# Retention gates by one Silu activation, and five pieces of a hybrid decoder kernel put elsewhere in the order of issue

## The chip, the cores and the metric

The kernel runs as one program on one core of a Trainium2 chip. The metric is the device time of an execution in microseconds (us). It is shown as the median of several runs. A profiled execution has a time of its own, beside the span from its first to its last instruction. The engines are TensorE (PE, with the weight loads as PEld), VectorE (DVE), ScalarE (ACT), GpSimd (POOL) and SyncE (SP). Each runs its own queue of instructions in order. An instruction waits on semaphores until what it needs is there, and everything behind it on its engine waits with it.

## The reference, cut to what matters

Two layers on x of 512 tokens by 1024 features, in float32. In each layer one projection makes the operands of two mixers and of two gates:

```python
h = rmsnorm(x, g_mix)
z = h @ w_in
aq, ak, av, rq, rk, rv, rg, ga, gb = jnp.split(z, SPLIT_POINTS, axis=-1)

aq = rope_half(aq.reshape(B, S, N_Q_HEADS, HEAD_DIM), pos)
ak = rope_half(ak.reshape(B, S, N_KV_HEADS, HEAD_DIM), pos)
ya = sliding_window_sink_attention(aq, ak, av, sinks) @ w_a

r = chunkwise_retention(rq, rk, rv)
r = r * lax.rsqrt(jnp.mean(r * r, axis=-1, keepdims=True) + EPS)
r = r.reshape(B, S, RET_V) * jax.nn.silu(rg.astype(jnp.float32))
yb = r.astype(x.dtype) @ w_b

mixed = jax.nn.sigmoid(ga) * ya + jax.nn.sigmoid(gb) * yb
x = x + mixed @ w_out
h2 = rmsnorm(x, g_mlp)
x = x + jnp.square(jax.nn.relu(h2 @ w_up)) @ w_down
```

Attention has 8 query heads over 2 key heads of 64, in bands of 128 queries, with a learned sink in the softmax. A last RMSNorm ends the program.

## The kernel before

Everything is kept transposed: features lie on the partitions and the 512 tokens along the free axis. A float32 matrix is brought to TensorE as two parts, a high one that ScalarE rounds (L342 for weights, L417 for values) and a low one that VectorE gets as the difference (L343 and L418). A product of two such operands is three matmuls, high by high (L394), low by high (L395) and high by low (L396). The weights come in units of 128 x 1024 that SyncE loads (`raw`) and `split_until` splits, `SPLIT` = 3 units ahead of the one in use. So the splits are spread through the queues of ScalarE and VectorE between all other work.

One layer goes through these stages. The projection in chunks of 128 features (`mm`), with attention's keys and queries first. `rotate` turns each (L638, L639, then L642 to L644 with tables that L633 scales by the row's norm); where its last argument is true, ScalarE first copies the bank of the result (L641), so that L642 reads the copy and not the bank. Then attention in four groups of two heads per key head and band, interleaved with the projection's other chunks: scores (L780), masked maximum (L788), exponential (L800), the sink's exponential (L803), scaling (L807), transposition of the weights (`pT`, L745), and the product with v (`pv`, L765 and L766), whose halves L767 and L768 put into `whole`. In the projection's chunks for the retention gate (`rg`), `put_rg` makes `z`, and `silu` applies the activation to it, eight times in a layer: four pieces at the end of attention, and four in the fast multiplication that makes the rest of the gates. Retention runs as a generator, `retention(pair)`, for two heads at a time: scores, outputs, norm and finish are steps between which other work is issued. The MLP is in blocks e of 512 hidden features, by a fast multiplication that uses sums and differences of operands (`sums`, `eu`, `b`); its result goes to memory by `Adding.put`, which adds the piece on VectorE (L1662) or sends it.

The order on each engine is set in three ways. The code issues chunks of the projection, and `advance` draws in a step of the background work (attention, retention) with each half of a chunk. A scheduler then places the instructions on each engine by priority as their operands and buffers come free. And `tc.issue_after(i)` holds what is issued in its block behind the named instruction i. `last_split` is the last split of attention's result (`whole`) into its halves, and `last_exp` the last exponential of the sink.

Three places are touched most. The tail of attention (L1176 to L1183): behind the last exponential `x`, which holds the gates a and b there, is passed through a sigmoid (L1178, two of 128 x 2048, with a table load), then come the first two `silu`; the other two come behind the last split. The keys of layer 1 (`put_k`, L671), where the bank of k's result is read by L642. The first MLP block, e = 0 (L1822 to L1824), where `rest` issues the last sum of inputs (L544) and its split (L417, L418) right after the block is issued.

Of the kernel before, what the change touches and what calls it, by code (L numbers as in the profile page):

```python
# [12 lines left out]
AF = mybir.ActivationFunctionType  # L13
ALU = mybir.AluOpType
# [38 lines left out]
SPLIT = 3  # L53
# [63 lines left out]
def decoder(ctx, tc, xT, x_first, w_in, w_rg, w_rv, w_a, w_b, w_wo, w_up, w_pair, w_down, w_end, tables, decay, band, g_last, out):  # L117
    nc = tc.nc
# [10 lines left out]
    def f32(ap):  # L129
        return ap.bitcast(F32)  # L130

    def temp(name="t"):
        return tmp.tile([P, T], F32, tag="t", name=name, bufs=7)

    def big(name, dtype=F32):
        return tmp.tile([P, 2, T], dtype, tag="big", name=name, bufs=6)
# [28 lines left out]
    state = {"next": 0, "loaded": 0, "split": 0, "hold": None}  # L165

    def halves(i):

        return (slice(0, UNIT // 2), slice(UNIT // 2, UNIT)) if i < 3 else (slice(0, UNIT),)
# [11 lines left out]
    def load_until(n):  # L181
        while state["loaded"] < min(n, len(order)):
            i = state["loaded"]
            layer, name, j = order[i][:3]
            if name == "pair":
                load_part(i)
            elif name == "block":
                load_block(i)
            elif name in MIXING:
                load_values(i)  # L190
            else:
                raws[i] = raw_tile()
                for at in halves(i):
                    queue = nc.scalar if i == 0 and at.start == 0 else nc.sync
                    source = w_end[j] if name == "w_end" else weights[name][layer, j]
                    queue.dma_start(raws[i][:, at], source[:, at])
                    if i < 3:
                        load_x()
            state["loaded"] += 1
# [79 lines left out]
    def add_part(i):  # L279
        if order[i][3] in (1, 2):  # L280
            last = raws.pop(i - 1)
            at = LEFT if order[i][3] == 1 else RIGHT
            nc.vector.tensor_tensor(raws[i][:, at], last[:, LEFT], last[:, RIGHT], ALU.add)  # L283
# [18 lines left out]
    def add_block(i):  # L302
        e, part = order[i][2:]
        if part in (2, 4) and e < N_BLOCK - 1:
            raws[i] = raws.pop(i - 2)
            nc.vector.tensor_tensor(raws[i], raws[i], raws.pop(i - 1), ALU.add)
# [10 lines left out]
    def add_values(i):  # L317
        name, part = order[i][1:3]
        if part in (2, 4):
            n = TALL[name]  # L320
            raws[i] = raws.pop(i - n)
            nc.vector.tensor_tensor(raws[i], raws[i], raws.pop(i - 2 * n), ALU.add)

    def split_until(n):
        while state["split"] < min(n, len(order)):
            i = state["split"]
            name, part = order[i][1], order[i][-1]
            if name in MIXING:
                add_values(i)
            load_until(i + AHEAD)  # L330
            if name == "pair":
                add_part(i)
            elif name == "block":
                add_block(i)
            raw = raws[i]
            hi = wpool.tile([P, UNIT], F32R, tag="hi", name="hi", bufs=SPLIT + 1)
            lo = wpool.tile([P, UNIT], F32R, tag="lo", name="lo", bufs=SPLIT + 1)
            for at in (LEFT,) if name == "pair" and part == 3 else halves(i):
                if i == 0 and at.start == 0:
                    nc.vector.tensor_copy(hi[:, at], raw[:, at])  # L340
                else:
                    state["high"] = nc.scalar.activation(hi[:, at], raw[:, at], AF.Copy).ins  # L342
                nc.vector.tensor_tensor(lo[:, at], raw[:, at], f32(hi[:, at]), ALU.subtract)  # L343
            kept = {
                "pair": part < 2,
                "block": name == "block" and part < 4 and order[i][2] < N_BLOCK - 1,
                **{n: name == n and order[i][2] < 4 for n in MIXING},
            }
            if not kept.get(name):
                raws.pop(i)  # L350
            parts[i] = (hi, lo)
            state["split"] += 1
# [268 lines left out]
    def layer_body(layer):  # L621
# [14 lines left out]
        def rotate(ps, tabs, early=False):  # L636
            a, b = temp("rot"), temp("rot2")
            nc.scalar.activation(b[0:64, :], ps[64:128, :], AF.Copy)  # L638
            nc.scalar.activation(b[64:128, :], ps[0:64, :], AF.Copy)  # L639
            if early:  # L640
                nc.scalar.activation(a, ps, AF.Copy)  # L641
            nc.vector.tensor_tensor(a, a if early else ps, tabs[0], ALU.mult)  # L642
            nc.vector.tensor_tensor(b, b, tabs[1], ALU.mult)
            nc.vector.tensor_tensor(a, a, b, ALU.add)  # L644
            return a
# [11 lines left out]
        attn_tabs, v_box = [], []  # L657
# [8 lines left out]
        def beside(g, stack, src):  # L666
            for s in range(2):
                own, other = 64 * s + 32 * g, 64 * s + 32 - 32 * g
                nc.sync.dma_start(f32(stack)[other : other + 32, :], f32(src)[own : own + 32, :])

        def put_k(ps):  # L671
            r = rotate(ps, attn_tabs, layer == 0)
            lo = big("klo")[:, 0, :]
            for g in range(N_KV):
                nc.scalar.activation(kh[g], r, AF.Copy)
            nc.vector.tensor_tensor(lo, r, f32(kh[0]), ALU.subtract)
            for g in range(N_KV):
                nc.vector.tensor_scalar(kl[g], lo, half[:, g : g + 1], None, ALU.mult)
                beside(g, kh[g], kh[g])
# [306 lines left out]
        rg, rg_next = {}, {}  # L986
# [71 lines left out]
            done(1)  # L1058

        def silu(i):  # L1060
            s = temp("sig")
            nc.scalar.activation(s, rg[i], AF.Sigmoid)
            nc.vector.tensor_tensor(rg[i], rg[i], s, ALU.mult)

        ret = {}

# [69 lines left out]
        def load_decay(pair):  # L1136
            decays[pair] = big("dm")
            nc.sync.dma_start(decays[pair], decay[:, 2 * pair : 2 * pair + 2, :])

        def retention(pair):  # L1140
            two = [Head(2 * pair), Head(2 * pair + 1)]
            for head in two:
                for js in ((0, 1), (2, 3)):
                    head.scores(js)
                    yield
            two[0].outputs(0)
            yield
            two[0].outputs(1)
            yield
            two[1].outputs(0)  # L1150
            yield
            yield
            two[0].norm()
            yield
            two[1].outputs(1)
            yield
            yield
            yield
            two[1].norm()
            if pair == 0:  # L1160
                load_decay(1)
            yield
            yield
            for head in two:
                head.finish()
                yield
# [9 lines left out]
        with tc.issue_after(last_exp[0]):  # L1176
            for hs in (slice(0, T // 2), slice(T // 2, T)):
                nc.scalar.activation(x[:, :, hs], x[:, :, hs], AF.Sigmoid)  # L1178
            for i in range(2):
                silu(i)  # L1180
        with tc.issue_after(last_split[0]), tc.issue_after(last_split[1]):
            for i in range(2, 4):
                silu(i)  # L1183
        turned.take()
# [7 lines left out]
        for u in range(4):  # L1192
            hi, lo = unit("w_a", layer)
            for j in range(2):
                c = 2 * u + j
                ps = bank(ps_mm, "mm")
# [447 lines left out]
        class Adding:  # L1644
# [14 lines left out]
            def put(self, i, j, m, ps, sign):  # L1659
                t = self.kept.pop((i, j, m), None)  # L1660
                if t is not None:
                    nc.vector.scalar_tensor_tensor(t, ps, self.scale(j, m, sign), t, ALU.mult, ALU.add)  # L1662
                else:
                    t = self.evacuated(j, m, temp("y"), ps, sign)
                self.send(i, j, m, t, last or self.e > 0)
# [138 lines left out]
        rest = []  # L1804
        for e in range(N_BLOCK):
            if e == 0:
                into = Adding(e)
                hooks = first_hooks()
                for c in (0, 2):
                    two_chunks("w_up", layer, xs, [put_up(c), put_up(c + 1)], hooks[c // 2])  # L1810
            else:
                plain = last and e == N_BLOCK - 1
                into = Ending() if e == N_BLOCK - 1 else Adding(e)
                if last and e == 2:
                    with tc.issue_after(state["high"]):
                        nc.scalar.activation(sq[:, 0:1], factor[:, 0:1], AF.Sqrt)
                pair(0)
                pair(1)
            if last and e == N_BLOCK - 1:
                down_plain(into)  # L1820
            else:
                down(e, into, None if e else lambda: rest.append(sum_input(2)))  # L1822
                if e == 0:
                    rest.pop()()  # L1824
        u_forms.free()
        slots.give(*u_two_slots, *u_one)

# [182 lines left out]
```

## Time and profile before

| what | value |
|---|---|
| median of three runs | 1462.46 us (1461.82 to 1465.33) |
| profiled execution | 1464.44 us |
| its span, first to last instruction | 1462.5 us |
| granted TensorE clock, mean | 0.999 |
| matmuls, us in them | 8185, 1449.4 |
| activations and loads on ScalarE | 974.0 us |
| VectorE | 1182.1 us |
| table loads on ScalarE | 17 of 1.283 us |

The profiled execution lies 1.98 us above the median of the three runs, and its span is 1.94 us shorter than its own time; all rows that follow are from this one execution. In its lists a row gives the start, the length and the instruction; behind "<-" stands what the engine waited for. The profile gives the time that an engine sat idle before an instruction in brackets. The pitch of matmuls, from one start to the next, shows what a wait cost better than the idle time alone does.

### The profile page before, as it was taken

To read this page: it belongs to the slowest core of one execution; us is meant where nothing else is said; L and a number is where in the kernel's file an instruction comes from. 1 tells how busy PE (TensorE), PEld (TensorE's weight loads), DVE (VectorE), ACT (ScalarE), POOL (GpSimd) and SP (SyncE) were. 2 spreads that over 40 slices of the span, in tenths; PEclk is the share of its full clock that TensorE was granted. 3 is DMA by queue.
4 is the path that set the end of the run, shared out by engine and by line. 5 is a ranking of instruction groups with operands and counts; after the bars stand their busy time and mean duration, and the time that the engine had idled before them with its cause. 6 is when DMAs were issued, how large, how long until landed. Compare 5 with 4: busy or idle time off the path is not lost.

```text
span 1462.5 us, 22466 instructions
## 1 busy us (share of the span) xinstructions
PE 1449.4 (99%) x8185; PEld 1270.0 (87%) x8185; DVE 1182.1 (81%) x1776; ACT 974.0 (67%) x1590; POOL 226.6 (15%) x335
## 2 busy tenths in 40 slices
PE   9999999999999999999999999999999999999998
PEld 7888888888988999999888889888889889999997
DVE  6978887867898888888778789878689888888885
ACT  6656665544687777777756576555447877777775
POOL 0011002222101111111201110012210011111120
PEclk9999999999999999999999999999999999999999
DMA  7598249999735777666955983599975477777664
GB/s 258 176 293 236 88 154 299 285 279 270 221 109 196 195 193 196 168 177 179 310 175 175 289 240 121 161 311 263 278 182 183 139 195 198 197 189 199 173 192 142
DMA packets 97294, 302.83 MB, mean 207 GB/s; under 512 B 11424, under 2 KB 11552, under 8 KB 90784
## 3 DMA queue, kind: packets, MB, share of 16 engines
q0 software_dynamic: 36512, 129.78, 37.9%
q1 hardware_dynamic: 59952, 170.32, 33.9%
q8 instruction: 64, 1.05, 0.3%
q10 hardware_dynamic: 720, 1.31, 0.2%
q14 instruction: 46, 0.38, 0.1%
HBM read 261.78 MB, written 120.06 MB: 261 GB/s over the span
## 4 chain that ended last, share of the span: by engine, by line
PE 96%; DVE 2%; ACT 1%; DMA 1%; issue 0%; DVEq 0%
PE mm L395 22%; PE mm L394 22%; PE mm L396 22%; PE wo L1354 5%; PE rg L1015 3%; PE b L394 3%; PE b L395 3%; PE b L396 3%; PE rv L395 2%; PE rv L394 2%; PE rv L396 2%; PE mm L410 2%; PE score L780 1%; PE pT L745 1%; PE r L395 1%; PE r L396 1%
## 5 line engine op out<-in xcount | busy, mean ns | idle before, releaser
L342 ACT ACTIVATE hi<-raw 128x1024 fp32r<-128x1024 f32 (+1 forms) x393 | 400.2, 1021 | 244.9 <-PE mm L395 122.3
L343 DVE TENSOR_TENSOR lo<-raw,hi 128x1024 fp32r<-128x1024 f32 (+1 forms) x394 | 460.2, 1176 | 96.4 <-ACT hi L342 93.0
L394 PE MATMUL mm<-xh,hi 128*128 128x512 f32 (+1 forms) x912 | 319.1, 354 | 1.6 <-DVE rot L642 0.6
L395 PE MATMUL mm<-xl,hi 128*128 128x512 f32 (+1 forms) x912 | 319.6, 353 | 0.0
L396 PE MATMUL mm<-xh,lo 128*128 128x512 f32 (+1 forms) x912 | 316.4, 353 | 0.5 <-DVE lo L343 0.5
L394 PEld LDWEIGHTS mm<-xh,hi 128*128 128x128 f32 x912 | 173.1, 190 | 25.6 <-ACT xh L420 1.2
L395 PEld LDWEIGHTS mm<-xl,hi 128*128 128x128 f32 x912 | 173.3, 190 | 21.9
L396 PEld LDWEIGHTS mm<-xh,lo 128*128 128x128 f32 x912 | 172.3, 190 | 21.8 <-DVE lo L343 0.7
L395 PE MATMUL mm<-r,hi 128*128 128x256 f32 (+1 forms) x608 | 189.3, 311 | 0.8 <-DVE r L418 0.8
L396 PE MATMUL mm<-r,lo 128*128 128x256 f32 (+1 forms) x608 | 189.0, 311 | 0.0
L394 PE MATMUL mm<-r,hi 128*128 128x256 f32 (+1 forms) x608 | 186.6, 312 | 0.5 <-ACT mm L1529 0.5
L394 PEld LDWEIGHTS mm<-r,hi 128*128 128x128 f32 x608 | 115.5, 190 | 9.9 <-ACT r L417 1.1
L395 PEld LDWEIGHTS mm<-r,hi 128*128 128x128 f32 x608 | 115.7, 190 | 9.6 <-DVE r L418 1.6
L396 PEld LDWEIGHTS mm<-r,lo 128*128 128x128 f32 x608 | 115.8, 190 | 6.3
L1677 POOL DMA_DIRECT2D y<-eu x56 | 63.0, 1397 | 372.2 <-DVE eu L1662 371.9
L395 PE MATMUL mm<-lo,r 128*128 128x512 f32 (+1 forms) x276 | 104.3, 387 | 0.0
L396 PE MATMUL mm<-hi,r 128*128 128x512 f32 (+1 forms) x276 | 100.9, 387 | 0.0
L394 PE MATMUL mm<-hi,r 128*128 128x512 f32 (+1 forms) x276 | 98.3, 389 | 0.3 <-ACT r L417 0.2
L394 PE MATMUL b<-hi,r 128*128 128x512 f32 x180 | 70.6, 392 | 1.9 <-DVE eu L1662 1.9
L283 DVE TENSOR_TENSOR raw<-raw 128x512 f32<-128x512 f32 x56 | 38.6, 690 | 41.2 <-DMA raw<-w_pair_in 35.1
L395 PE MATMUL b<-lo,r 128*128 128x512 f32 x180 | 70.2, 390 | 0.0
L1354 PE MATMUL wo<-r,hi 128*128 128x256 f32 x384 | 69.2, 283 | 0.0
(337 smaller groups left out, 2870.9 us busy)
## 6 DMA issues: line engine op xcount, KB each, us to landing
raw<-w_in_in SPq DMA_DIRECT2D x65, 512.0 KB, 5.5
sums_down<-w_down_in POOLq DMA_DIRECT2D x30, 1024.0 KB, 12.9
sums_up<-w_pair_in POOLq DMA_DIRECT2D x56, 512.0 KB, 12.0
raw<-w_down_in SPq DMA_DIRECT2D x45, 512.0 KB, 7.5
raw<-w_pair_in SPq DMA_DIRECT2D x84, 256.0 KB, 3.6
y<-y POOLq DMA_DIRECT2D x62, 256.0 KB, 9.9
y<-eu POOLq DMA_DIRECT2D x61, 256.0 KB, 8.7
raw<-sums_down SPq DMA_DIRECT2D x30, 512.0 KB, 7.7
```

Source lines behind the costliest of these rows:

```text
L283: nc.vector.tensor_tensor(raws[i][:, at], last[:, LEFT], last[:, RIGHT], ALU.add)
L342: state["high"] = nc.scalar.activation(hi[:, at], raw[:, at], AF.Copy).ins
L343: nc.vector.tensor_tensor(lo[:, at], raw[:, at], f32(hi[:, at]), ALU.subtract)
L394: nc.tensor.matmul(ps, ah, bh, start=start and i == 0, stop=False, **more)
L395: nc.tensor.matmul(ps, ah, bl, start=False, stop=False, **more)
L396: latest[0] = nc.tensor.matmul(ps, al, bh, start=False, stop=stop and i == n - 1, **more).ins
L410: latest[0] = nc.tensor.matmul(ps, w[:, cols(j, c)], moving[k][low], start=first, stop=bool(final)).ins
L745: nc.tensor.transpose(pt[:, i * P : (i + 1) * P], sm[:, at : at + P], ident)
L780: nc.tensor.matmul(ps[:, g * w : (g + 1) * w], q_s[g][:, c, at], part[:, keys], start=i == 0, stop=i == 1)
L1015: nc.tensor.matmul(o, w[:, cols], v, start=start and k == 0 and n == 0 and w is hi and v is vh, stop=k == 3 and n == 1 and w is lo, skip_g ...
L1354: latest[0] = nc.tensor.matmul(o, w[:, cols], v, start=start and first and n % 2 == 0 and w is hi and v is vh, stop=final and w is lo, ski ...
L1677: nc.gpsimd.dma_start(y[:, 2 * j + m, i * T : (i + 1) * T], t, **how)
```

## The change

There are five edits. `silu` becomes one activation in place, Silu, where a Sigmoid and a multiplication stood. In the tail of attention, one more unit of weights is split behind the last split of attention, ahead of the last two `silu`. In `retention`, the norm of the first two heads comes after the fourth head's outputs, not between third and fourth. `put_k` passes True, so that the bank of the keys is copied in layer 1 too, where only layer 0 did it before. And `Adding.put` keeps the addition in `self.added`, and the last sum of the first MLP block is issued behind it.

```diff
         def put_k(ps):
-            r = rotate(ps, attn_tabs, layer == 0)
+            r = rotate(ps, attn_tabs, True)
...
         def silu(i):
-            s = temp("sig")
-            nc.scalar.activation(s, rg[i], AF.Sigmoid)
-            nc.vector.tensor_tensor(rg[i], rg[i], s, ALU.mult)
+            nc.scalar.activation(rg[i], rg[i], AF.Silu)
...
             two[1].outputs(0)
             yield
             yield
-            two[0].norm()
-            yield
             two[1].outputs(1)
             yield
+            two[0].norm()
             yield
             yield
             two[1].norm()
...
         with tc.issue_after(last_split[0]), tc.issue_after(last_split[1]):
+            split_until(state["next"] + SPLIT + 1)
             for i in range(2, 4):
                 silu(i)
...
             def put(self, i, j, m, ps, sign):
                 t = self.kept.pop((i, j, m), None)
                 if t is not None:
-                    nc.vector.scalar_tensor_tensor(t, ps, self.scale(j, m, sign), t, ALU.mult, ALU.add)
+                    self.added = nc.vector.scalar_tensor_tensor(
+                        t, ps, self.scale(j, m, sign), t, ALU.mult, ALU.add
+                    ).ins
...
                 if e == 0:
-                    rest.pop()()
+                    with tc.issue_after(into.added):
+                        rest.pop()()
```

These edits move the order of instructions at several places. In the rows, numbers behind a name are those of buffers; they differ between the two programs. Line numbers behind the edits shift by two or three.

On ScalarE at the keys of layer 1, the bank of k, `mm_7310` before and `mm_7294` after, is read by L638 and L639. Before:

```order
L638 ACTIVATE rot2_7534<-mm_7310 64x512
L639 ACTIVATE rot2_7534<-mm_7310 64x512
L417 ACTIVATE sh_7490<-wide_7488 128x512
L342 ACTIVATE hi_7583<-raw_7444 128x1024
L342 ACTIVATE hi_7629<-raw_7450 128x1024
L616 ACTIVATE rstd_7524<-ssq_7525 128x512
```

And after:

```order
L638 ACTIVATE rot2_7518<-mm_7294 64x512
L639 ACTIVATE rot2_7518<-mm_7294 64x512
L641 ACTIVATE rot_7517<-mm_7294 128x512
L417 ACTIVATE sh_7474<-wide_7472 128x512
L638 ACTIVATE rot2_7538<-mm_7296 64x512
L639 ACTIVATE rot2_7538<-mm_7296 64x512
L342 ACTIVATE hi_7568<-raw_7428 128x1024
```

The copy L641 now stands right behind L639, and the rotation of the next chunk, `mm_7296`, comes ahead of two splits of weights.

On VectorE in the first MLP block of layer 0, L1662 (L1660 after) adds the four evacuated pieces `eu`. Before:

```order
L544 SCALAR_TENSOR_TENSOR sums_4148<-sums_4147,xg_4144 128x512
L418 TENSOR_TENSOR r0_81<-sums_3989,r0_81 128x512
L283 TENSOR_TENSOR raw_4154<-raw_4122 128x512
L343 TENSOR_TENSOR lo_4125<-raw_4023,hi_4124 128x1024
L418 TENSOR_TENSOR r1_82<-sums_4147,r1_82 128x1024
L343 TENSOR_TENSOR lo_4157<-raw_4078,hi_4156 128x1024
L1662 SCALAR_TENSOR_TENSOR eu_4140<-mm_4074,columns_3899,eu_4140 128x512
L418 TENSOR_TENSOR r4_85<-sums_4148,r4_85 128x1024
L1662 SCALAR_TENSOR_TENSOR eu_4142<-mm_4075,columns_3899,eu_4142 128x512
L1662 SCALAR_TENSOR_TENSOR eu_4118<-b_4076,columns_3899,eu_4118 128x512
L1662 SCALAR_TENSOR_TENSOR eu_4120<-b_4077,columns_3899,eu_4120 128x512
```

And after:

```order
L418 TENSOR_TENSOR r1_82<-sums_4131,r1_82 128x1024
L343 TENSOR_TENSOR lo_4141<-raw_4062,hi_4140 128x1024
L1660 SCALAR_TENSOR_TENSOR eu_4124<-mm_4058,columns_3883,eu_4124 128x512
L1660 SCALAR_TENSOR_TENSOR eu_4126<-mm_4059,columns_3883,eu_4126 128x512
L1660 SCALAR_TENSOR_TENSOR eu_4102<-b_4060,columns_3883,eu_4102 128x512
L343 TENSOR_TENSOR lo_4165<-raw_4082,hi_4164 128x1024
L1660 SCALAR_TENSOR_TENSOR eu_4104<-b_4061,columns_3883,eu_4104 128x512
L544 SCALAR_TENSOR_TENSOR sums_4132<-sums_4131,xg_4128 128x512
L343 TENSOR_TENSOR lo_4189<-raw_4106,hi_4188 128x1024
L343 TENSOR_TENSOR lo_4212<-raw_4138,hi_4211 128x1024
L283 TENSOR_TENSOR raw_4208<-raw_4184 128x512
L418 TENSOR_TENSOR r4_85<-sums_4132,r4_85 128x1024
```

The sum (L544) and its split, `r4_85`, now stand behind the last of the four.

On ScalarE at the end of attention in layer 1, from the last exponential of the sink (L803) on. Here `x_75` holds the two gates, `z` with `sig` or alone the retention gate, `whole` the result of attention, and `pT` the transposed weights. Before:

```order
L803 ACTIVATE st_8400<-st_8400 128x2
L1178 ACT_TABLE_LOAD
L1178 ACTIVATE x_75<-x_75 128x8x256 x2
L417 ACTIVATE late_7390<-rot_8447 128x512
L767 ACTIVATE whole_8411<-pv_8412 64x512
L767 ACTIVATE whole_8411<-pv_8419 64x512
L1062 ACTIVATE sig_8634<-z_8505 128x512
L417 ACTIVATE r3_84<-pT_8428 128x4x128
L1062 ACTIVATE sig_8637<-z_8505 128x512
L342 ACTIVATE hi_8648<-raw_8507 128x1024
L417 ACTIVATE r6_87<-whole_8411 128x4x128
L417 ACTIVATE r3_84<-pT_8467 128x4x128
```

And after:

```order
L803 ACTIVATE st_8385<-st_8385 128x2
L1175 ACT_TABLE_LOAD
L1175 ACTIVATE x_75<-x_75 128x8x256 x2
L1061 ACT_TABLE_LOAD
L1061 ACTIVATE z_8490<-z_8490 128x512 x2
L417 ACTIVATE r6_87<-whole_8396 128x4x128
L417 ACTIVATE late_7374<-rot_8432 128x512
L638 ACTIVATE rot2_8655<-mm_8629 64x512
L639 ACTIVATE rot2_8655<-mm_8629 64x512
L417 ACTIVATE r3_84<-pT_8452 128x4x128
L417 ACTIVATE r3_84<-pT_8471 128x4x128
L417 ACTIVATE r3_84<-pT_8511 128x4x128
```

The Silu of the first two pieces stands with a table load right behind the gates, and the halves of `pT` come behind more work; the weight split `hi_8648` and the two halves of `whole` are no longer between them. On TensorE, 82 matmuls of 512 columns and 16 of 128 stand from the last scores to the next product with v there before, and 56 and 16 after; the seven chunk matmuls that stood between the last product with v and the retention matmuls behind it stand ahead of that product now.

The program's table loads become 21.

## The prediction

> **What bounds the kernel now.** I read the page first, for the engine shares and the chain that ended last, then TensorE's waits, then the timelines around each wait and around the places that the change reorders. Three lines of the page:
>
> ```profile
> span 1462.5 us, 22466 instructions
> PE 1449.4 (99%) x8185; PEld 1270.0 (87%) x8185; DVE 1182.1 (81%) x1776; ACT 974.0 (67%) x1590; POOL 226.6 (15%) x335
> PE 96%; DVE 2%; ACT 1%; DMA 1%; issue 0%; DVEq 0%
> ```
>
> TensorE is busy for 99% of the span and is 96% of the chain. Its work isn't touched: it has 8185 matmuls and keeps them. So the change can gain only what TensorE waits for, and lose only by making it wait elsewhere. VectorE, at 81%, and ScalarE, at 67%, matter only where they are late. The waits of TensorE (total us, times, longest) are these:
>
> ```profile
> PE b L394 <- DVE eu L1662: 1.9, 2, 1.2
> PE mm L394 <- DVE rot L642: 0.6, 1, 0.6
> ```
>
> Few microseconds are to be had. A wait is larger in the pitch of the matmuls than in this list, since the first matmul behind it runs longer, so I count by start times. A matmul of 512 columns starts every 0.227 us in an undisturbed stretch, one of 256 columns every 0.12, one of 128 every 0.11; these three come from the starts in the stretches below and beside them.
>
> **The Silu itself.** Sixteen sigmoid activations become sixteen Silu activations, and sixteen multiplications go.
>
> ```profile
> L1062 ACT ACTIVATE sig<-z 128x512 f32<-128x512 f32 x16 | 9.3, 620 | 1.1 <-DVE z L1034 1.0
> L1063 DVE TENSOR_TENSOR z<-z,sig 128x512 f32<-128x512 f32 x16 | 10.6, 685 | 0.1
> ...
> 852.73 1.28 ACT L1178 ACT_TABLE_LOAD   x1
> ```
>
> On VectorE 10.6 us of work go. That is no gain of time by itself, because TensorE waits for neither row. On ScalarE the number stays. Silu has no row in the trace; from one pass like the sigmoid (0.62) up to sigmoid and multiplication together (0.62 + 0.69 = 1.31) is what I allow, and I take 0.62, since every one-pass activation of this shape in the trace lies near it. The program has 21 table loads where it had 17, so ScalarE gets 4 x 1.28 = 5.1 us more. Two of them (second half of retention in each layer) stand in stretches where ScalarE idles behind TensorE; their cover is ScalarE's 33% idle time, and without it they would cost 1.28 each. The other two stand in the tail of attention, once per layer, on ScalarE's path there.
>
> **Keys of layer 1.** The stall goes as follows (start, duration, row):
>
> ```profile
> 763.99 0.39 PE L396 MATMUL mm<-xh,lo 128*128 128x512 f32 x1
> 765.01 0.50 PE L394 MATMUL mm<-xh,hi 128*128 128x512 f32 x1 [0.63 <-DVE rot L642]
> 765.34 0.39 PE L395 MATMUL mm<-xl,hi 128*128 128x512 f32 x1
> ...
> 763.00 1.22 DVE L633 TENSOR_TENSOR tab<-rawtab,rstd 128x1024 f32<-128x1024 f32 x1 [2.34 <-ACT rstd L616]
> 764.26 0.69 DVE L642 TENSOR_TENSOR rot<-mm,tab 128x512 f32<-128x512 f32 x1
> ```
>
> The chunk at 765.01 waits for the bank that L642 still reads, and L642 waits for the tables of L633. Excess: (1.02 - 0.227) + (0.33 - 0.227) = 0.90. With the early copy ScalarE empties the bank right behind L639, and L642 reads the copy; so the bank is free well before L633 starts at 763.00. That costs ScalarE one more activation of 512 columns, some 0.62, which its idle time there hides (the 2.34 us that VectorE waits for L616 are idle on ScalarE too, since L616 waits for TensorE). Term: -0.90 (bounds 0 and -0.90).
>
> **Retention's fourth head.** The stall of layer 1 stands where TensorE wants the first two heads' gated output:
>
> ```profile
> 1056.07 0.39 PE L396 MATMUL mm<-xh,lo 128*128 128x512 f32 x1
> 1056.51 1.20 PE L394 MATMUL mm<-r,hi 128*128 128x512 f32 x4
> 1057.85 0.50 PE L394 MATMUL mm<-xh,hi 128*128 128x512 f32 x1
> 1058.19 0.40 PE L395 MATMUL mm<-xl,hi 128*128 128x512 f32 x1
> ```
>
> Excess: (0.44 - 0.227) + (1.34 - 0.91) + (0.34 - 0.227) = 0.75. In the new order the norms stand closer together and the products on these halves stand later in TensorE's queue; following the rows I find them ready over 4 us before they are wanted. The fourth head's outputs, issued earlier, are followed by enough matmuls. Term: -0.75 (bounds 0 and -0.75).
>
> **First MLP block, layer 0.**
>
> ```profile
> 445.27 0.39 PE L396 MATMUL b<-hi,r 128*128 128x512 f32 x1
> 445.71 0.39 PE L394 MATMUL mm<-xh,hi 128*128 128x256 f32 x1
> 445.93 0.28 PE L395 MATMUL mm<-xl,hi 128*128 128x256 f32 x1
> 447.41 0.50 PE L394 MATMUL b<-hi,r 128*128 128x512 f32 x1 [1.20 <-DVE eu L1662]
> 447.75 0.39 PE L395 MATMUL b<-lo,r 128*128 128x512 f32 x1
> ...
> 444.81 1.22 DVE L418 TENSOR_TENSOR r<-sums,r 128x1024 fp32r<-128x1024 f32 x1
> 446.61 1.41 DVE L1662 SCALAR_TENSOR_TENSOR eu<-b,columns,eu 128x512 f32<-128x512 f32 x2
> ```
>
> The product at 447.41 waits for a bank that L1662 reads at 446.61. Excess: 0.21 + 0.10 + 1.36 + 0.11 = 1.78. The change puts the sum L544 (0.6 by the pitch of such rows) and L418 (1.13, from 444.81 to the next start) behind the four evacuations, so the one at 446.61 moves to about 444.9. What becomes late is the split of that sum: it is done near 452.7, and TensorE wants it near 456.3. Term: -1.75 (bounds -1.78 and 0).
>
> **First MLP block, layer 1.** The same stall, then what follows:
>
> ```profile
> 1172.57 0.39 PE L396 MATMUL b<-hi,r 128*128 128x512 f32 x1
> 1173.23 0.39 PE L394 MATMUL mm<-xh,hi 128*128 128x256 f32 x1 [0.28 <-ACT hi L342]
> 1173.46 0.28 PE L395 MATMUL mm<-xl,hi 128*128 128x256 f32 x1
> 1174.45 0.50 PE L394 MATMUL b<-hi,r 128*128 128x512 f32 x1 [0.71 <-DVE eu L1662]
> 1186.55 0.39 PE L396 MATMUL mm<-xh,lo 128*128 128x256 f32 x1 [0.46 <-DVE lo L343]
> ...
> 1176.21 0.33 SPq L273 DMA_DIRECT2D raw<-w_pair_in  x1
> ...
> 1184.67 0.69 DVE L283 TENSOR_TENSOR raw<-raw 128x512 f32<-128x512 f32 x1 [5.01 <-DMA raw<-w_pair_in]
> ...
> DMA to landing us min/median/max: 4.2/7.5/11.5
> ```
>
> Excess: 0.43 + 0.11 + 0.87, and 0.1 behind as at 447.75, 1.5, saved in the same way. But now the sum's L418 stands behind the L283 that waited 5.01 us for a transfer issued at 1176.21, 8.4 us before. Behind that L283 now stand L418, a split of 512 (0.6) and one of 1024 (1.13), which TensorE wants at 1183.9 to 1184.5. The buffer comes free earlier, so the issue moves to 1173.8; with 8.4 us and 0.6 for traffic it lands at 1182.8, the last low half is ready near 1186.4, and 1.9 are lost, where 1.0 was lost at 1186.55 (0.46 of it in the row) and just behind before. Term: -1.5 - 1.0 + 1.9, about -0.5. If it lands when it did, 1.8 more are lost, about +1.3; without any wait it is -2.5.
>
> **Tail of attention.** In layer 0 one split goes behind the last one of attention and the wait at its end, 0.95, stays by the rows (I get 0.99): +0.05. In layer 1 the order changes more, and here lies the loss. Before:
>
> ```profile
> 848.59 0.64 PE L780 MATMUL score<-r,r 128*128 128x256 f32 x4
> 869.52 0.39 PE L765 MATMUL pv<-r,r 128*128 128x512 f32 x1
> 876.32 0.51 PE L395 MATMUL mm<-r,hi 128*128 128x512 f32 x1 [0.38 <-DVE r L418]
> ...
> 852.53 0.19 ACT L803 ACTIVATE st<-st 128x2 f32<-128x2 f32 x1
> ...
> 854.02 3.72 ACT L1178 ACTIVATE x<-x 128x2048 f32<-128x2048 f32 x2
> 863.60 1.58 ACT L417 ACTIVATE r<-pT 128x512 fp32r<-128x512 f32 x3 [0.98 <-PE pT L745]
> ...
> 854.10 1.28 DVE L995 TENSOR_TENSOR z<-mm,rstd 128x512 f32<-128x512 f32 x2
> 864.23 1.89 DVE L418 TENSOR_TENSOR r<-pT,r 128x512 fp32r<-128x512 f32 x3
> ```
>
> From the end of the last scores (849.07) to the last product with V (869.52) TensorE had 82 matmuls of 512 and 16 of 128 columns, 18.6 + 1.8 = 20.4 us; the operands were there at 866.1, 3.4 us early. Now it has 56 and 16: 12.7 + 1.8 = 14.5 us. The chain against it: VectorE reaches the sum for L803 4.2 us after the scores, since its last masks and scalings (1.7, as before), two L995 (1.28) and L642, L643 (1.2) stand ahead; then ScalarE needs 0.2 (L803) + 1.28 + 3.72 (gates) + 1.28 (Silu's load) + 1.05 (two Silu, 0.52 apart as in the row of 863.60) + 1.05 (two splits) + 1.2 (L638, L639, each like L1062) + 1.6 (three splits of pT) = 11.4, up to 15.6; VectorE, with a rotation among its last low halves, is done at 17.7. The product that reads that half comes at 15.1, so TensorE waits 2.6, about 2.85 with its restarts. After these products seven chunk matmuls (1.59) that covered the split of the result now stand ahead; the wait of 0.95 at 876.32 becomes about 2.4. Together 2.85 + 2.4 - 0.95 = +4.3. Its bounds: 0, if the walk has lost the slack that it finds, and +5.7 with Silu at 1.31 twice.
>
> The Trainium skill ("ScalarE: Activation LUTs", section "What ACT_TABLE_LOAD costs") gives a switch of tables about 1.28 us of load and about 1.38 of drain, 2.66 in all. Here the load ends at 854.01 and the activation behind it starts at 854.02, so this trace shows the first part and no drain; by the page's figure this term would be 1.4 larger, an estimate from that page.
>
> **Sum.** -0.90 - 0.75 - 1.75 - 0.5 + 0.05 + 4.3 = +0.45, on the profiled execution's 1464.44: 1464.9. That execution lies 2.0 above the median of the three runs, 1462.46, so in terms of the median the forecast is 1462.9. About 0.3%, 4.4 us, is what a measurement of this kernel can tell from no change.
>
> **Rivals.** Chances are for the whole case; times are against the median.
> - *The tail of layer 1 costs nothing* (0.25). For it: the same chain had 3.4 us of slack before. Against it: 5.9 us of cover go, and a load and a rotation join. 0.45 - 4.3 = -3.85: 1458.6; with layer 1's transfer not waited for either, -5.85: 1456.6. In half of this case the time is faster by over 0.3%.
> - *The transfer decides* (0.15, mostly slower). VectorE now waits with the sum's split behind the L283 of layer 1. If its issue stays at 1176.21 and takes the longest landing of the stretch, 11.5, it comes at 1187.7, 4.9 later than I took: +0.45 + 4.9 = 5.35, 1467.8. It makes the kernel slower by over 0.3% once it lands after 1186.8. For it: the wait of 5.01. Against: the slot that the transfer needs is read earlier.
> - *The savings don't come* (0.10): the copies and the evacuations move, but TensorE finds another wait right behind each. Without the terms of the keys, the norms and the first blocks, +0.05 + 4.3: 1466.8, at the bound. Against: the rows behind each place show slack of 1 us and more.
> - *A load is dearer than its row* (0.07): a pause of the size of the load behind the one in the tail, +1.3: 1464.2. The Trainium skill's drain, above, would be this case; 854.01 and 854.02 speak against it.
>
> My forecast, no change, has 0.43. Slower by over 0.3% gets 0.12 from the transfer and 0.04 from the missing savings and 0.01 from the load; faster gets 0.13 from the tail; the rest, 0.70, lies within. The range, 1457.8 to 1467.8, reaches from the tail without cost to the late transfer.
>
> **What would show it.** TensorE's waits lose the rows for L1662 and for L642, and a wait for L417 or L418 of pT appears before the last products with V of layer 1, and a larger one behind them. Around 765 and 1056 matmuls keep 0.227. Near 1184 VectorE waits at L283 with TensorE behind it. ScalarE shows 21 table loads. I am wrong if the tail of layer 1 shows no wait, if a Silu takes over 0.7 us, or if a place that I found free holds TensorE for over 2 us.

## The result: 0.16% slower, inside the range, with two errors that cancel

The changed kernel takes 1465.09 us (median of 17 runs, 1463.41 to 1467.29) where the kernel before takes 1462.46 (17 runs, 1461.63 to 1465.33). The ratio is 1.0016, interval 1.0009 to 1.0023. So it is a little slower, by less than the 0.3% within which the prediction called it unchanged; the forecast was 1462.9. Runs of one kernel often fall into two groups some 2 us apart (before, 1461.6 to 1462.8 and 1463.4 to 1465.3), which the section on the hardware comes back to; the ratios are over all runs.

The page of the kernel after:

```profile
span 1461.9 us, 22453 instructions
PE 1447.1 (99%) x8185; PEld 1269.2 (87%) x8185; DVE 1176.5 (80%) x1760; ACT 979.1 (67%) x1595; POOL 228.0 (16%) x335
PE 96%; ACT 2%; DVE 1%; issue 0%; DMA 0%; ACTq 0%; DVEq 0%
```

VectorE is busy for 5.6 us less, ScalarE for 5.1 more, and TensorE is as full as before. What moved is in TensorE's waits (total, times, longest):

```profile
PE ret L394 <- DVE whole L768: 1.9, 1, 1.9
PE pv L765 <- DVE r L418: 1.3, 1, 1.3
...
PE pv L766 <- DVE r L418: 0.7, 1, 0.7
PE mm L394 <- ACT r L417: 0.7, 2, 0.5
```

The rows for the additions of the MLP (L1662 before, L1660 now) and for L642 are gone. In their place stand three waits in the tail of layer 1's attention. The timeline of TensorE there:

```profile
851.67 0.64 PE L780 MATMUL score<-r,r 128*128 128x256 f32 x4
...
866.57 0.39 PE L396 MATMUL mm<-xh,lo 128*128 128x512 f32 x1
868.29 1.01 PE L765 MATMUL pv<-r,r 128*128 128x512 f32 x2 [1.33 <-DVE r L418]
870.00 0.50 PE L766 MATMUL pv<-r,r 128*128 128x512 f32 x1 [0.70 <-DVE r L418]
...
871.50 0.40 PE L929 MATMUL rv<-xh,ones 128*128 128x512 f32 x1
873.76 0.50 PE L394 MATMUL ret<-late 128*128 128x512 f32 x1 [1.86 <-DVE whole L768]
...
875.51 1.06 PE L394 MATMUL mm<-r,hi 128*128 128x512 f32 x2
876.37 0.63 PE L395 MATMUL mm<-r,hi 128*128 128x512 f32 x1
876.79 0.63 PE L396 MATMUL mm<-r,lo 128*128 128x512 f32 x1
...
878.07 0.40 PE L396 MATMUL mm<-r,lo 128*128 128x512 f32 x1
878.30 0.39 PE L394 MATMUL mm<-r,hi 128*128 128x512 f32 x1
```

From 871.50 to 873.76 stand 2.26 us where a pitch of 0.227 would do. Behind that the pitch itself is 0.43 for three microseconds, with no wait shown. ScalarE's queue for the same tail:

```profile
856.27 0.20 ACT L803 ACTIVATE st<-st 128x2 f32<-128x2 f32 x1 [0.44 <-DVE st L798]
856.49 1.28 ACT L1175 ACT_TABLE_LOAD   x1
857.78 3.72 ACT L1175 ACTIVATE x<-x 128x2048 f32<-128x2048 f32 x2
861.51 1.28 ACT L1061 ACT_TABLE_LOAD   x1
862.80 1.15 ACT L1061 ACTIVATE z<-z 128x512 f32<-128x512 f32 x2
...
866.24 1.57 ACT L417 ACTIVATE r<-pT 128x512 fp32r<-128x512 f32 x3
```

The chain is as the prediction laid it out: L803 comes 4.1 us behind the scores (which end at 852.14), and the halves of pT are done 11.5 us behind L803.

To compare stages, I add up for each kernel's profile by how much the pitch of TensorE's matmuls exceeds the undisturbed one (0.227 us at 512 columns, 0.120 at 256, and so on), in stretches of the program. This is worked out from all start times of the timeline; it is no view of the profile.

| us lost on TensorE | before | after | difference | predicted |
|---|---|---|---|---|
| start, first 13 us | 4.80 | 2.41 | -2.39 | - |
| tail of attention, layer 0 | 1.04 | 1.32 | +0.28 | +0.05 |
| first MLP block, layer 0 | 1.81 | 0.10 | -1.71 | -1.75 |
| keys, layer 1 | 1.07 | 0.10 | -0.97 | -0.90 |
| tail of attention, layer 1 | 1.16 | 6.93 | +5.77 | +4.3 |
| retention's fourth head, layer 1 | 1.02 | 0.20 | -0.82 | -0.75 |
| first MLP block, layer 1 | 2.74 | 0.84 | -1.90 | -0.5 |
| all other stretches | 7.06 | 6.84 | -0.22 | 0 |
| behind the last matmul, to the end of the span | 6.21 | 7.42 | +1.21 | 0 |

The edited places and the rest, without the start, sum to +0.43 us up to the last matmul; the prediction's sum was +0.45. The start differs between executions of one kernel, and the two profiles happen to differ there; that is why the span after is shorter than before although the time is longer. The medians differ by 2.63 us, more than 0.43 and 1.21 make together. The profiled execution of the changed kernel is the third fastest of its 17 runs, with a mean clock of 0.998 where ten of the others show 0.996 or 0.997; so the half clock behind the waits probably takes more in a usual execution than in this one.

### The profile page after: what moved, and what is told of

It is laid out like the page before. It is cut to its first block, busy times and chain, and to the rows that moved or that the text cites. A ratio compares the mean times of both kernels' runs of the same rounds, so it can differ in the third digit from the quotient of the medians.

```text
span 1461.9 us, 22453 instructions
## 1 busy us (share of the span) xinstructions
PE 1447.1 (99%) x8185; PEld 1269.2 (87%) x8185; DVE 1176.5 (80%) x1760; ACT 979.1 (67%) x1595; POOL 228.0 (16%) x335
## 4 chain that ended last, share of the span: by engine, by line
PE 96%; ACT 2%; DVE 1%; issue 0%; DMA 0%; ACTq 0%; DVEq 0%
PE mm L394 22%; PE mm L396 22%; PE mm L395 22%; PE wo L1352 5%; PE b L394 3%; PE b L395 3%; PE b L396 3%; PE rg L1015 3%; PE rv L396 2%; PE rv L394 2%; PE rv L395 2%; PE mm L410 2%; PE score L780 1%; PE pT L745 1%; PE r L396 1%; PE r L395 1%
## 5 line engine op out<-in xcount | busy, mean ns | idle before, releaser
L394 PE MATMUL b<-hi,r 128*128 128x512 f32 x180 | 70.5, 392 | 0.0
L396 PE MATMUL b<-hi,r 128*128 128x512 f32 x180 | 67.6, 389 | 0.0
```

The source lines that it names most:

```text
L394: nc.tensor.matmul(ps, ah, bh, start=start and i == 0, stop=False, **more)
L396: latest[0] = nc.tensor.matmul(ps, al, bh, start=False, stop=stop and i == n - 1, **more).ins
```

## The experiments

### The keys alone, and all but the keys

The prediction charged the keys with a gain of 0.9 and left the tail's new order to the change as a whole. At the old pace the scheduler puts 82 matmuls of 512 columns ahead of the last products with v in each of the seven kernels here where the keys of layer 1 stay as they were, and 56 or 57 in each where they are copied early. So the keys were taken back, and then tried alone.

```diff
-            r = rotate(ps, attn_tabs, True)
+            r = rotate(ps, attn_tabs, layer == 0)
```

> The changed kernel with the keys of layer 1 rotated from the bank, as before; the other four edits stay. Theory (the copy L641 of layer 1 sets the new order of the tail of layer 1's attention): the waits before the last products with V and for L768 in layer 1 go, as does the half clock behind them; a wait of about 1.3 us as in layer 0 stays, the wait of 0.9 for L642 at 765 comes back. Sum against before: -1.79 - 2.03 - 0.75 + 0.3 + 0.3 = -4.0, about 1458.5 us. Rival (the Silu with its table load and the moved split make the tail's loss): the waits stay, 4 us or more; about 1464.5 to 1466 us.

It took 1459.9 us beside 1463.99 of the kernel before on the same chip: ratio 0.9979 (0.9970 to 0.9987). Its tail of layer 1 loses 1.54 us, not 6.93. The kernel before with the keys' line of the change alone:

> The kernel before with the early copy of layer 1's keys alone. Theory: the tail of layer 1 is reordered, with waits before the last products with V and behind them; less than in the changed kernel, as one table load (1.28) is not in the chain; 2 to 5 us lost there, 0.9 saved at 765: 1463.5 to 1466.5 us. Rival: the copy saves its 0.9 and nothing else: 1461.5 us.

1467.27 us, ratio 1.0023 (1.0014 to 1.0033). TensorE's waits of that run:

```profile
PE ret L394 <- DVE whole L768: 1.9, 1, 1.9
PE b L394 <- DVE eu L1662: 1.9, 2, 1.2
...
PE mm L394 <- DVE z L995: 1.0, 1, 1.0
```

The wait for L768 is there without Silu and without the moved split, the wait for L642 is gone, and the tail loses 5.34 us. There is no wait at the products with v, which fits the shorter chain without the Silu's load. The cause of the loss in the tail is the edit to the keys. It costs 0.23% alone and 0.37% on top of the other four edits (1.0016 against 0.9979), so the effects of the edits don't simply add.

### What the early copy does: its order, or its 0.6 us

Two runs were to say how the copy does it. In the first, the changed kernel draws in attention's steps faster in layer 1, which puts 80 matmuls ahead of the last products with v.

```diff
-            chunk("w_in", layer, xs, put_gate(c), PACE)
+            chunk("w_in", layer, xs, put_gate(c), (PACE, 0.85)[layer])
...
-        qk(0, PACE)
+        qk(0, (PACE, 0.85)[layer])
...
-            chunk("w_in", layer, xs, put_rg(i), PACE)
+            chunk("w_in", layer, xs, put_rg(i), (PACE, 0.85)[layer])
```

> The changed kernel with the background steps of layer 1's attention drawn in at a rate of 0.85 per half chunk where it was 0.8; in its order 80 matmuls of 512 columns stand between the last scores and the last products with V where 56 stood. Theory (the lost cover makes the waits before those products, 2.86 us): these waits go; the wait for L768 of about 1.9 and the half clock behind it (1.6) stay, since only one matmul covers it as before. 1465.1 - 2.9 = 1462.2 us. Rival (the copy makes the data itself late): the waits stay within 0.5 us, 1465 us.

It took 1464.91 us, ratio 1.0014 (1.0005 to 1.0022), beside the changed kernel again at 1464.99:

> The changed kernel again, on the chip of the three others, for comparison with the run with the faster pace: 1.7 to 2.5 us over the kernel before, with the waits at the same places: 2.9 before the last products with V of layer 1, 2.1 for L768, and 1.6 in matmuls at a pitch of 0.427 behind it.

That run gave 1.0016 (1.0007 to 1.0025). Of what was expected of its waits, those before the last products with v came again, but the wait for L768 was 0.59 and the half pitch stood ahead of it; the section on the hardware shows why. With the faster pace the waits before the last products went, as foretold; but as much came back at the group before:

```profile
847.76 0.74 PE L780 MATMUL score<-r,r 128*128 128x256 f32 x4 [0.66 <-DVE st L788]
850.06 0.80 PE L765 MATMUL pv<-r,r 128*128 128x512 f32 x1 [1.57 <-ACT r L417]
850.65 0.63 PE L394 MATMUL mm<-xh,hi 128*128 128x512 f32 x1
```

and the wait for L768 was 2.4, where the changed kernel had 1.9. The clock fell behind both places, for 3.41 us each time. So cover is what the waits before the last products lacked, which speaks against the rival, late data; but moving cover does not make more of it. That each group's chain of softmax needs as much cover as before, and some group meets TensorE with too little, fits the rows and wasn't tried.

In the second, VectorE makes the copy, on top of the norm and MLP edits.

```diff
             if early:
-                nc.scalar.activation(a, ps, AF.Copy)
+                nc.scalar.activation(a, ps, AF.Copy) if early is True else nc.vector.tensor_copy(a, ps)
...
-            r = rotate(ps, attn_tabs, layer == 0)
+            r = rotate(ps, attn_tabs, True if layer == 0 else "other")
```

> Norm and MLP edits with the keys of layer 1 copied early by VectorE instead of ScalarE. Theory (it is the bank coming free early that lets the scheduler put the projection's chunks ahead, whoever copies; 57 matmuls of cover in the tail): the tail of layer 1 loses 3 to 5 us against the two edits alone, 1462 to 1464 us, the wait at 765 goes or shrinks. Rival (the copy's 0.6 us on ScalarE delays attention there): no loss in the tail, 1458.5 us.

1466.02 us, ratio 1.0017 (1.0008 to 1.0026), while the two edits alone give 0.9977: the stretch of the tail loses 8.00 us, more than foretold. But the largest wait is another one. VectorE:

```profile
849.30 1.23 DVE L633 TENSOR_TENSOR tab<-rawtab,rstd 128x1024 f32<-128x1024 f32 x1 [4.77 <-DMA rawtab<-tables_in]
```

Here the transfer of retention's tables is issued at 835.08 (825.70 in the changed kernel), and VectorE waits for it, with TensorE behind. That wait (3.15 us by the pitch) and the half clock behind it (1.6) make some 4.7 of the 8.00. So time is lost when VectorE makes the copy too, which speaks for the order and against the rival; but the run doesn't isolate the lost cover, since its order moved a transfer as well. Whether the bank coming free early could be had with the old order was not run.

### The Silu alone

```diff
-            s = temp("sig")
-            nc.scalar.activation(s, rg[i], AF.Sigmoid)
-            nc.vector.tensor_tensor(rg[i], rg[i], s, ALU.mult)
+            nc.scalar.activation(rg[i], rg[i], AF.Silu)
```

> The kernel before with the Silu alone. Theory (Silu costs one pass like the sigmoid, its extra table load in the tail of attention is covered by the slack of 3.4 us that the tail has in the old order): within 0.5 us of before, 1462.5 to 1464, with the waits of 0.95 at the end of both attentions about as they were. Rival (the load is on the path of the tail): a new wait of 1 to 2 us before the last products with V in each layer, 2 to 4 us more.

1465.21 us, ratio 1.0015 (1.0007 to 1.0024). Neither theory foretold this. No wait before the products with v appears, so the load isn't on that path. But the wait behind them grows, in layer 1 as follows on TensorE, and on ScalarE ahead of the row that it waits for:

```profile
875.40 0.96 PE L394 MATMUL mm<-r,hi 128*128 128x512 f32 x3 [1.36 <-ACT r L417]
```

```profile
870.37 1.27 ACT L767 ACTIVATE whole<-pv 64x512 f32<-64x512 f32 x2 [0.22 <-PE pv L766]
872.41 1.06 ACT L342 ACTIVATE hi<-raw 128x1024 fp32r<-128x1024 f32 x1 [0.77 <-PE mm L395]
873.50 0.60 ACT L638 ACTIVATE rot<-mm 64x512 f32<-64x512 f32 x1
874.11 0.59 ACT L639 ACTIVATE rot<-mm 64x512 f32<-64x512 f32 x1
874.72 0.63 ACT L417 ACTIVATE r<-whole 128x512 fp32r<-128x512 f32 x1
```

The split of the result (L417) stands behind a weight split and a rotation (L638, L639); in the kernel before, the rotation came behind it. The tails lose 0.9 us each more than before (1.94 and 2.04), and 0.6 more go at the first MLP block of layer 1, against 0.4 saved at retention's fourth head. VectorE's 10.6 us bought nothing that shows.

### The moved split alone

```diff
         with tc.issue_after(last_split[0]), tc.issue_after(last_split[1]):
+            split_until(state["next"] + SPLIT + 1)
             for i in range(2, 4):
                 silu(i)
```

> The kernel before with the moved weight split alone. Theory (the split, 1.06 us on ScalarE, now comes behind the last split of attention and the product behind waits for it): the wait of 0.95 at the end of both attentions becomes 1.2 to 1.3 with a second wait for L342, +0.6 us in all. Rival (the split ahead of the last one was what held the last one up): the wait for L418 gets shorter by 0.5 or more in each layer, 1 us or more gained.

1462.93 us, ratio 1.0001 (0.9992 to 1.0010): the same. The rival was right about the wait and wrong about the gain. The wait of 0.95 is gone from both tails (0.03 and 0.25 are lost there), and a new one, for a weight split, stands some 30 us further on in each layer:

```profile
PE rv L394 <- ACT hi L342: 2.1, 2, 1.0
```

### The norm alone, the MLP alone, and both

The two edits are those of the diff above, each on the kernel before.

> The kernel before with the norm behind the fourth head's outputs, alone. The prediction's term: 0.75 us less at 1056 and nothing elsewhere, 1461.7 us. Rival (that wait depends on where TensorE stands, since it was absent with the Silu alone and with the moved split alone): it goes, and as much comes back elsewhere in the same layer: 1462.5 us.

1462.39 us, ratio 0.9998 (0.9989 to 1.0007). The 0.8 us at 1056 are saved in its profile (0.23 lost there, 1.02 before), but the time can't tell it from none. The same wait was absent with the split alone too (0.20), so it hangs on where TensorE stands, and not on this edit alone.

> The kernel before with the sum of the first MLP block behind the last addition, alone. Theory (this edit carries nearly all of the gain of the two edits tried together): 1.7 us at the first block of layer 0 and 1.5 to 2 in layer 1, 3.3 to 3.7 in all: 1458.8 to 1459.2 us. Rival (the two edits need each other, or the norm carries its own part): 2.5 us or less.

1460.25 us, ratio 0.9976 (0.9965 to 0.9986). Its waits:

```profile
PE mm L395 <- DVE r L418: 0.8, 2, 0.4
PE mm L394 <- ACT xh L420: 0.7, 1, 0.7
PE mm L394 <- DVE rot L642: 0.6, 1, 0.6
```

None is left for the additions, and the first blocks lose 0.04 and 0.16 us where they lost 1.81 and 2.74.

> The kernel before with two edits: the norm behind the fourth head's outputs, and the sum of the first MLP block behind its last addition. Theory: -0.75 - 1.79 - 2.03 = -4.6 us, about 1457.9 us, and no row for L1660 among the waits of TensorE. Rival (the savings come back as other waits at once): within 1 us of before, 1461.5 to 1463.5 us.

1459.72 us, ratio 0.9977 (0.9967 to 0.9987), no better than the MLP edit alone within the interval. With the Silu and the moved split added, which is the changed kernel without the keys' copy, the ratio was 0.9979: the loss that the Silu brings alone doesn't show there, where the weight split no longer stands ahead of L417. So one edit of five carries the gain, and the three kernels that have it, keep the keys as they were and keep the old pace beat both kernels of this case.

### A faster pace on the better kernel

The norm and MLP edits, with the pace of layer 1 at 0.87, by the same three lines as above.

> Norm and MLP edits, and the background steps of layer 1's attention drawn in at 0.87 per half chunk where it was 0.8: 76 matmuls of 512 columns ahead of the last products with V where 82 stood, 7 among them and 10 behind them where 2 and 8 stood. Theory (cover behind the last products ends the wait of 0.95 there, and 6 fewer ahead stay within the slack of 3.4 us): 0.5 to 0.9 us less than the two edits alone, about 1459.0 us. Rival (a wait appears at an earlier group of attention, as with the faster pace of the changed kernel): 1 to 3 us more than the two edits alone.

1466.4 us, ratio 1.0021 (1.0012 to 1.0030): more than the rival's loss, and at another place than a group of attention. The theory failed too, as the wait of 0.95 behind the last products stayed. VectorE:

```profile
853.37 1.22 DVE L633 TENSOR_TENSOR tab<-rawtab,rstd 128x1024 f32<-128x1024 f32 x1 [5.23 <-DMA rawtab<-tables_in]
```

SyncE issues that transfer at 844.04, where the kernel before does at 825.64; TensorE waits 4.9 us behind it, and the clock is at a half for 6.83 us.

### Work in the wait

The half pitch behind the wait for L768 was taken for a lower clock. Eight matmuls more of a placeholder, whose result isn't used, were put into that wait:

```diff
-            nc.tensor.matmul(b[1], ones, xh[:, 0, :], start=True, stop=True)
+            for _ in range(9 if layer else 1):
+                nc.tensor.matmul(b[1], ones, xh[:, 0, :], start=True, stop=True)
```

> The changed kernel with the placeholder matmul of 128x512 (L929) in layer 1 issued nine times where it stands once; its result isn't used, and the eight more run in the wait of 1.86 us for L768. Theory (idle time lowers the granted clock just behind it): the matmuls behind the wait keep a pitch of 0.227 us where they had 0.427; 1.6 us less than the changed kernel, about 1463.5 us. Rival (the pitch belongs to these matmuls, or to a transfer beside them): the pitch stays 0.427 and the time stays at 1465.1 us, or rises by up to 1.8.

1465.26 us, ratio 1.0010 (1.0001 to 1.0019). The interval overlaps that of the changed kernel, so the time alone decides nothing. The timeline shows more:

```profile
873.99 2.23 PE L930 MATMUL rv<-xh,ones 128*128 128x512 f32 x9
876.25 0.50 PE L394 MATMUL ret<-late 128*128 128x512 f32 x1
876.59 0.39 PE L395 MATMUL ret<-late 128*128 128x512 f32 x1
...
877.64 0.73 PE L394 MATMUL mm<-r,hi 128*128 128x512 f32 x2
878.37 0.50 PE L395 MATMUL mm<-r,hi 128*128 128x512 f32 x1
878.70 0.40 PE L396 MATMUL mm<-r,lo 128*128 128x512 f32 x1
```

The same matmuls keep their pitch, and the tail loses 4.04 us beside the 1.8 that the fillers themselves take, 5.9 where the changed kernel loses 6.93. Only 1.1 of the 1.6 us come back by this account, since the fillers take part of the time that the clock gives. One profile doesn't settle it, as the repetition of the changed kernel had no half pitch behind this wait either, but the mean clocks of all executions help. In the kernels whose profile shows no half clock in mid-program they are 0.999 or 1.000 in nearly every run. The changed kernel has 0.999 in one of 28 runs and 0.996 to 0.998 in the others; with the fillers it is 0.999 in six of 11 and 0.997 in five, and these five lie 1.4 us above the six in the mean. So idle time there does lower the clock, and filling the longest wait keeps it up in about half of the executions only.

## Why the prediction was right, and where it was wrong

**The bound.** Right in the main. TensorE's 8185 matmuls set the time, and the gains and losses show as waits of TensorE, but for two that the prediction had no term for: the half clock, and the time behind the last matmul.

**Silu.** 0.62 us was right (9.2 us for 16, 0.619 each), and so were the 21 loads, but not whose they are. The Silu alone has 17: two more in the tails and two fewer in layer 1's retention. The norm alone has 19. Against the kernel before, the two loads in retention are both in layer 0 (six where four stood), not one in each layer. The cost of nothing outside layer 1's tail was wrong for the Silu by itself: alone it costs 0.15%, by the order of ScalarE's queue behind the products with v. Layer 0's tail lost 0.28, not 0.05.

**Keys.** The term of -0.90 was right where it was looked for (-0.97). The step that failed is that the edit ended there: it was charged 0.6 us of ScalarE, hidden, while the order that follows from it in the next 100 us cost 5.39 (the tail loses 6.93 with it and 1.54 without). The tail's term held most of that cost, without the edit that makes it.

**Fourth head.** -0.75 foretold, -0.82 measured. But alone the edit gives no time that could be measured, and the wait also goes without it.

**First MLP blocks.** Layer 0 was right (-1.75, -1.71). In layer 1 the mechanism was right and the size off. VectorE does wait at L283, and L418 stands behind it:

```profile
1180.73 0.69 DVE L283 TENSOR_TENSOR raw<-raw 128x512 f32<-128x512 f32 x1 [2.48 <-DMA raw<-w_pair_in]
1181.34 1.22 DVE L418 TENSOR_TENSOR r<-sums,r 128x1024 fp32r<-128x1024 f32 x1
...
1174.15 0.33 SPq L273 DMA_DIRECT2D raw<-w_pair_in  x1
```

The transfer was issued 2.1 us earlier, as said, but landed 6.6 us later and not 9.0. So the low halves were in time, TensorE lost nothing there, and the edit gave 1.4 more than predicted. In the repetition of the changed kernel the landing took 7.4 and the block lost about 0.7 more, so a part of that gain belongs to this one execution.

**Tail of layer 1.** +4.3 foretold, +5.77 measured. The waits before the last products were foretold at 2.85; they are 2.85 (1.49 + 0.28 + 0.97 with 0.11 of restart, by the pitch). The wait behind was foretold at 2.4 (0.95 and the lost 1.59 would make 2.5) and is 2.1, at the bank of the retention matmul rather than at the split. What was missing is 1.6 us of matmuls at half the clock. The tail's term and that of layer 1's MLP block were off by 1.5 and 1.4 in opposite directions. That the sum of the stretches came out is luck; the medians moved by 2.63 where +0.45 was forecast.

**The load's drain.** Here the second load starts at 861.51, takes 1.28, and the Silu behind it starts at 862.80. The 1.38 us of drain that the Trainium skill ("ScalarE: Activation LUTs", section "What ACT_TABLE_LOAD costs") adds to a switch do not show, as they didn't before; the rival that rested on it fell.

**Behind the last matmul.** 1.21 us are lost where the prediction had nothing: 7.42 in the profile of the changed kernel, 7.43 and 7.42 in its repetition and with the fillers, 6.2 to 6.7 in the others. The last transfers of the result are issued 2.7 us behind the last matmul before and after, so the difference lies behind their issue. I have no experiment on it, and the cause stays open.

## What to carry to other kernels

When a list scheduler orders the work, an edit that frees a buffer early is an edit to all that follows it: price it by the order of the next stage, with a count of the matmuls that cover each chain there, not by its own instructions. When five edits are timed together, the sum hides the good ones: here one gives 0.24%, three give nothing or a little loss, and one eats the gain. A wait on a saturated TensorE can cost more than its length, so that the longest, and those which stand close together, are the ones to remove first.

## What the runs showed of the hardware

The half clock was not expected. The granted clock of the changed kernel by stretches (it is the first number behind the busy times of PE, PEld, DVE, ACT and POOL):

```profile
866.00:872.00 6.00, 3.84 (x14) 2.06 (x12) 5.66 (x10) 4.50 (x9) 1.22 (x2) 1.00 0.75 150
872.00:874.60 2.60, 0.83 (x4) 0.59 (x5) 2.54 (x5) 0.42 (x2) 0.00 (x0) 1.00 0.30 58
874.60:878.20 3.60, 3.60 (x11) 3.05 (x11) 2.58 (x4) 3.60 (x6) 0.57 (x1) 0.53 0.24 60
878.20:884.00 5.80, 5.80 (x28) 4.78 (x27) 5.20 (x7) 5.64 (x9) 0.00 (x0) 1.00 0.67 238
```

By the trace's own record of the clock it falls to a half at 874.63, for 3.41 us, and comes back. The other falls in mid-program were as long, or twice that: 3.41 in five more, in four profiles, and 6.83 in one. In the repetition of the same kernel it fell at another place, behind the first two waits:

```profile
871.50:874.20 2.70, 2.70 (x7) 1.79 (x6) 2.70 (x6) 0.95 (x3) 0.00 (x0) 0.53 0.87 156
```

In the profile with the fillers, the same first two waits were followed by no such fall. A single wait of 1.4 us (the Silu alone) brought none either: its 11 executions have clocks of 0.999 and 1.000. But in the run with the keys alone a fall of 3.41 us follows a single wait of 1.93 us, the only one within 16 us:

```profile
876.02 0.50 PE L394 MATMUL ret<-late 128*128 128x512 f32 x1 [1.93 <-DVE whole L768]
```

The Trainium skill ("TensorE: Matmul & The Clock Gate", section "Part 1: The HAM clock gate") says that the clock is judged by activity in windows of about 3.4 us that run freely and don't start anew with the kernel. The length of the fall and its changing place agree. Its rule against idle gaps of over 3.4 us doesn't: with the keys alone one wait of 1.93 us was enough, and in the changed kernel waits of 1.9 us or less, two or three together.

The clock at the start goes with the two groups of times. The first matmuls of a profile run at a pitch of 0.43, and the first 13 us lose 2.4 to 2.8 us in six of the 14 profiles, 3.2 and 3.4 in two, and 4.7 to 4.9 in six, by how long they do; the profile of before is of the last kind, that of after of the first. In the seven kernels whose profiles show no half clock in mid-program and no fillers, the profiled time lies in the group that its start says. A comparison of two single profiles has to leave the start out.
